# Computing the right half of row blocks 2 and 3 by Strassen while B streams in

## The chip, the cores and the metric

The kernel runs on one core of one Trainium2 chip. The metric is the device time of one execution in microseconds (us). All times are medians over several executions. The span that a profile gives is about 1.8 us shorter than the device time of the same execution, so spans are compared with spans and times with times.

Engine names: PE is the matrix engine, DVE the vector engine, ACT the scalar engine, POOL the GpSimd engine, SP the sync engine, which here only issues DMA transfers.

## The reference

```python
m, k, n = 2048, 2048, 2048           # a: m x k, b: k x n, gamma: n, all float32; eps = 1e-5

def reference(a, b, gamma, eps):
    x = np.matmul(a, b)
    rms = np.sqrt(np.mean(x ** 2, axis=-1, keepdims=True) + eps)
    return (gamma * x / rms).astype(np.float32)
```

A matrix product, then every row is divided by its root mean square and multiplied by gamma.

## The kernel before

The rows of A come in 16 blocks of 128. Row blocks 0 to 3 ("the head") are computed with plain bf16 matmuls while B streams in: a first stage for the left half of B's columns and a second stage for the right half. After that B stands in the core's memory, and groups of two row blocks follow: group g holds row blocks 2g and 2g+1, for g = 2 to 7. (The prediction calls g = 2 the first group; where a quoted expectation says third group, it is g = 3, with row blocks 6 and 7; g = 4 has row blocks 8 and 9.) A group has a left and a right half of the columns, and each half is one step of Strassen's method: seven products of 8 matmuls instead of eight. A product accumulates in a bank of PE's accumulation memory (the tile `acc`, 128 x 512 float32); ACT and DVE take the banks out and combine them.

There are eight tiles of 1024 float32 columns; the head fills all eight, and later row blocks reuse them, so a tile can be overwritten only when the store of the old row block has left it:

```python
x_slot = [consts.tile([P, HALF], FP32, name=f"x_{n}") for n in range(8)]
# ...
def x_tile(mb, h):
    if (mb, h) not in x_half:
        n = n_x[0]
        n_x[0] += 1
        if n < 8:
            slot = n
        else:
            g = n // 4
            slot = ((0, 4, 1, 5), (0, 1, 4, 5))[g // 2 % 2 == 0][n % 4] + 2 * (g % 2)
        x_half[mb, h] = x_slot[slot]
    return x_half[mb, h]
```

By this rule the left tile of row block 7 is tile 6, which held the right half of row block 2.

How a row block leaves: scaled in place by DVE, stored by SP, 512 KB per half.

```python
def finish(mb, order=(0, 1)):
    # ... (rms and its inverse)
    for h in order:
        x = x_half.pop((mb, h))
        nc.vector.scalar_tensor_tensor(
            out=x, in0=x, scalar=r, in1=gamma_sb[:, h * HALF:(h + 1) * HALF],
            op0=ALU.mult, op1=ALU.mult)
        nc.sync.dma_start(out=rows(mb, h * HALF, (h + 1) * HALF), in_=x)
```

Half a group, with "hooks" at which other work is put in, and the loads of the A blocks for the group after next. `t` is a scratch area that is only an alias of the result chunk `x22`, so the first ACT copy of a half writes into a tile that may still be on its way out:

```python
def group_half(g, j, hooks):
    # ...
    t = x22
    at_hook(0)
    p2, p5 = new_bank(), new_bank()
    product(g, j, 2, p2)
    c = spare if (g, j) == (G0, 0) else t        # G0 = 2
    nc.scalar.copy(out=c, in_=p2)
    last_squares()
    at_hook(1)
    product(g, j, 5, p5)
    nc.vector.tensor_tensor(out=t, in0=p5, in1=c, op=ALU.add)
    at_hook(2)
    p1 = new_bank()
    product(g, j, 1, p1)
    nc.vector.tensor_tensor(out=t, in0=p1, in1=t, op=ALU.subtract)
    at_hook(3)
    product(g, j, 4, p2, start=False)            # needs p2 copied out
    nc.scalar.copy(out=x21, in_=p2)
    # ... (products 3, 7, 6)

def load_after(g, mb):
    wait_for(x_chunk(2 * g + 1, 1)[:, 0:1])      # POOL reads one column, then issues
    load_block(mb)

def hooks_of(g, j):
    # ...
    if j == 0:
        if g == G0:
            # ...
            hook(2, finish, 1)
            hook(3, squares2, 2)
            hook(4, apply, nxt + 1)
            hook(4, finish, 2)                   # row block 2 leaves: LEFT half of g = 2
    else:
        # ...
        if g + 2 < NG:
            hook(0, load_after, g, nxt + 2)      # loads of blocks 2g+4, 2g+5: RIGHT half
            hook(0, load_block, nxt + 3)
            hook(5, row_norm, nxt + 2)
```

## Time and profile before

| | kernel before |
|---|---|
| device time, median | 224.48 us (three runs, 224.18 to 224.62) |
| span of the profiled execution | 222.6 us |
| PE busy | 211.1 us, 95% |
| PE waiting, all entries | 3.5 us, all before 24.7 us |
| one 512-column matmul, start to start | 215.8 ns |

From the page of the kernel before: the first line gives each engine's busy time, its share of the span and its number of instructions, the second each engine's share of the span in the chain of waits that ended last.

```profile
PE 211.1 (95%) x1043; PEld 98.6 (44%) x1043; DVE 161.8 (73%) x324; ACT 129.1 (58%) x272; POOL 24.5 (11%) x49
...
PE 83%; DMA 8%; DVE 2%; POOL 2%; issue 1%; ACT 1%; DVEq 0%; ACTq 0%; POOLq 0%
```

PE is the limit: followed back from the end, 83% of the span is PE's own work. The list of PE's waits in the kernel before (line, what it waited for, total us, times, longest us) has only four entries:

```profile
PE acc L138 <- DVE sq L129: 1.5, 1, 1.5
PE tbank L148 <- POOL msq L198: 1.2, 1, 1.2
PE acc L350 <- DMA b<-in_b_dram: 0.4, 1, 0.4
PE tbank L382 <- DVE head_at L170: 0.4, 1, 0.4
```

All lie at the start. So from 24.7 us on, PE never waits; a change gains only by taking matmuls away, and loses by every wait that it makes.

The timeline of PE in the kernel before, in the groups (start, duration, line, what, count). Line 279 is a Strassen product: 69.25 is the first product of group 2, 84.84 product 1 of its right half and 86.57 product 4.

```profile
69.25 3.62 PE L279 MATMUL acc<-b,s 128*128 128x512 bf16 x16
...
84.84 1.89 PE L279 MATMUL acc<-early,s 128*128 128x512 bf16 x8
86.57 3.77 PE L279 MATMUL acc<-early,at_even 128*128 128x512 bf16 x16
...
97.08 1.89 PE L279 MATMUL acc<-t_left,s 128*128 128x512 bf16 x8
98.81 3.62 PE L279 MATMUL acc<-t_left,head_at 128*128 128x512 bf16 x16
102.26 7.07 PE L279 MATMUL acc<-b,s 128*128 128x512 bf16 x32
```

No line carries a bracket, that is, no idle time before it. Next, when the A blocks 8 and 9 are asked for:

```profile
88.37 1.06 POOL L115 DMA_DIRECT2D a<-in_a_dram  x2 [0.32 <-issue]
```

### The profile page before, as it was taken

The page shows a single profiled execution, that of the slowest core. Times are in us where ns is not written, and L with a number is a line of the kernel's source. Part 1 is how long each engine was busy: PE and PEld are TensorE (multiplying, and loading weights), DVE is VectorE, ACT ScalarE, POOL GpSimd, SP SyncE. Part 2 cuts the span into 40 slices and gives each one's busy share as a digit, 9 for nine tenths or more (in the row PEclk, how much of TensorE's full clock was granted, in tenths as well). Part 3 has the DMA queues.
Part 4 walks back from the last instruction along what each step waited for, and adds up shares of the span by engine and source line. Part 5 has one row for each costly group of instructions (what it writes and reads, how often), then busy time and mean ns, then how long its engine had stood idle before and what let it go on. Part 6 is the DMA issues. An engine that isn't in the chain of part 4 may idle for free.

```text
span 222.6 us, 3026 instructions
## 1 busy us (share of the span) xinstructions
PE 211.1 (95%) x1043; PEld 98.6 (44%) x1043; DVE 161.8 (73%) x324; ACT 129.1 (58%) x272; POOL 24.5 (11%) x49
## 2 busy tenths in 40 slices
PE   7899999999999999999999999999999999999950
PEld 2445444444454444444444444444444444444430
DVE  2427557983999989978949298837994589587692
ACT  3110002807698895799646985699478954334570
POOL 7534232300000001000100002000200000000000
PEclk9999999999999999999999999999999999999997
DMA  6999999999973499818889259945994794044045
GB/s 184 223 202 209 203 208 211 212 303 259 327 280 159 188 272 292 310 72 226 276 228 400 58 174 222 366 151 143 246 368 168 97 282 189 0 188 193 0 190 188
DMA packets 36176, 47.13 MB, mean 212 GB/s; under 512 B 21952, under 2 KB 26048, under 8 KB 34496
## 3 DMA queue, kind: packets, MB, share of 16 engines
q0 software_dynamic: 9648, 23.33, 41.6%
q1 hardware_dynamic: 26080, 22.29, 33.0%
q10 hardware_dynamic: 432, 1.31, 2.0%
q8 instruction: 8, 0.13, 0.2%
q14 instruction: 8, 0.07, 0.1%
HBM read 34.60 MB, written 16.78 MB: 231 GB/s over the span
## 4 chain that ended last, share of the span: by engine, by line
PE 83%; DMA 8%; DVE 2%; POOL 2%; issue 1%; ACT 1%; DVEq 0%; ACTq 0%; POOLq 0%
PE acc L279 63%; PE acc L350 18%; DMA b<-in_b_dram 8%; POOL early L106 1%; DVE x L617 1%; POOL b L100 1%; DVE x L620 1%; PE tbank L179 1%; PE tbank L382 1%; PE tbank L165 1%; ACT sq L291 0%; DVEq L732 0%; ACT sq L682 0%; DVE x L690 0%; DVE r L322 0%
## 5 line engine op out<-in xcount | busy, mean ns | idle before, releaser
L279 PE MATMUL acc<-b,s 128*128 128x512 bf16 x376 | 83.3, 379 | 0.0
L279 PEld LDWEIGHTS <-s 128*128 128x128 f16 x472 | 46.2, 98 | 55.7 <-DVE s L244 0.2
L350 PE MATMUL acc<-b,head_at 128*128 128x512 bf16 x240 | 55.1, 379 | 0.6 <-DMA b<-in_b_dram 0.4
L291 ACT ACTIVATE sq<-x 128x512 bf16<-128x512 f32 x62 | 39.1, 631 | 10.9 <-DVE x L520 5.1
L340 DVE SCALAR_TENSOR_TENSOR x<-x,r,gamma_sb 128x1024 f32<-128x1024 f32 x28 | 34.7, 1282 | 0.8
L209 ACT ACTIVATE sq<-a 128x1024 bf16<-128x1024 f32 x24 | 25.4, 1057 | 16.8 <-DMA a<-in_a_dram 16.4
L350 PEld LDWEIGHTS <-head_at 128*128 128x128 bf16 x240 | 22.9, 98 | 26.7 <-issue 1.1
L393 ACT COPY x<-acc 128x512 f32<-128x512 f32 x11 | 5.9, 591 | 25.1 <-PE acc L350 25.1
L231 ACT ACTIVATE head_at<-a,s 128x2048 f16<-128x2048 f32 x10 | 19.9, 1990 | 0.0
L279 PEld LDWEIGHTS <-at_even 128*128 128x128 f16 x96 | 9.4, 98 | 11.5 <-issue 0.4
L279 PEld LDWEIGHTS <-head_at 128*128 128x128 f16 x96 | 9.4, 98 | 11.3
L100 POOL DMA_DIRECT2D b<-in_b_dram x15 | 10.6, 708 | 16.0 <-DMA b<-in_b_dram 13.2
L217 DVE TENSOR_SCALAR s<-norm 128x1 f32<-128x1 f32 x12 | 1.8, 150 | 14.3 <-ACT norm L212 14.2
L244 DVE TENSOR_TENSOR s<-at_even 128x1024 f16<-128x1024 f16 x15 | 9.7, 684 | 2.8 <-DMA at_even<-head_at 2.8
L291 ACT ACTIVATION_READ_ACCUMULATOR sq<-x 128x1 f32 x62 | 11.7, 188 | 0.0
L279 PE MATMUL acc<-t_left,s 128*128 128x512 bf16 x48 | 11.3, 379 | 0.0
L279 PE MATMUL acc<-early,s 128*128 128x512 bf16 x48 | 11.3, 379 | 0.0
L279 PE MATMUL acc<-early,at_even 128*128 128x512 bf16 x48 | 11.0, 379 | 0.0
L279 PE MATMUL acc<-t_left,at_even 128*128 128x512 bf16 x48 | 10.9, 379 | 0.0
L509 ACT COPY x<-acc 128x512 f32<-128x512 f32 x10 | 5.7, 575 | 8.9 <-PE acc L279 8.9
L279 PE MATMUL acc<-t_left,head_at 128*128 128x512 bf16 x48 | 10.8, 379 | 0.0
L279 PE MATMUL acc<-early,head_at 128*128 128x512 bf16 x48 | 10.8, 379 | 0.0
(86 smaller groups left out, 205.8 us busy)
## 6 DMA issues: line engine op xcount, KB each, us to landing
out_dram<-x SPq DMA_DIRECT2D x30, 512.0 KB, 3.1
a<-in_a_dram POOLq DMA_DIRECT2D x12, 1024.0 KB, 8.5
b<-in_b_dram POOLq DMA_DIRECT2D x15, 512.0 KB, 17.1
early<-in_a_dram POOLq DMA_DIRECT2D x7, 256.0 KB, 14.8
early<-in_b_dram ACTq DMA_DIRECT2D x2, 512.0 KB, 5.9
gamma_sb<-in_gamma_dram POOLq DMA_DIRECT2D x1, 1024.0 KB, 19.9
out_dram<-x SPq DMA_DIRECT2D x3, 256.0 KB, 3.5
early<-in_a_dram SPq DMA_DIRECT2D x1, 512.0 KB, 5.7
```

The costliest lines, as they stand in the source:

```text
L100: nc.gpsimd.dma_start(out=raw[j][kp], in_=b[kp * W2:(kp + 1) * W2, j * HALF:(j + 1) * HALF].rearrange("(t p) n -> p t n", p=P))
L106: nc.gpsimd.dma_start(out=ah(kp), in_=a[0:HB * P, kp * W2:(kp + 1) * W2].rearrange("(r p) k -> p r k", p=P))
L165: nc.tensor.matmul(view[:, t, r, :], ah(kp)[:, r, t * P:(t + 1) * P], identity, is_transpose=True, start=(t == 0 and r == 0), stop=(t == 1 ...
L209: nc.scalar.activation(out=junk, in_=a32[mb][:, h * HALF:(h + 1) * HALF], func=ACTF.Square, scale=2.0 ** -8, accum_out=n2[:, h:h + 1])
L231: nc.scalar.activation(out=a16[mb], in_=a32.pop(mb), func=ACTF.Copy, scale=factor.pop(mb))
L244: nc.vector.tensor_tensor(out=s_sum[s], in0=x, in1=y, op=op)
L279: nc.tensor.matmul(bank, lhsT[:, kp, :], rhs, start=(start and kp == 0), stop=(kp == KP - 1), skip_group_check=not start)
L291: nc.scalar.activation(out=sq[:, 0:CH], in_=src, func=ACTF.Square, scale=inv_sqrt_n, accum_out=msq[mb][:, c:c + 1])
L340: nc.vector.scalar_tensor_tensor(out=x, in0=x, scalar=r, in1=gamma_sb[:, h * HALF:(h + 1) * HALF], op0=ALU.mult, op1=ALU.mult)
L350: nc.tensor.matmul(bank, head_at[:, kt, r, :], head_rhs(c, kt), start=(kt == 0), stop=(kt == KT - 1))
L393: copy(out=x_chunk(*g), in_=banks[g])
L509: nc.scalar.copy(out=x21, in_=p2)
```

## The change

Intent: the right half of row blocks 2 and 3 is also done by Strassen ("the pair"), with its products 2, 5 and 1 accumulated while B's right half streams in. That is 56 matmuls for 64. To make room, A blocks 4 and 5 are no longer transposed within the second stage and after it, but at the end of the pair. The first group gets a new order: row block 0 is scaled in two parts, row block 1 and blocks 6 and 7 come at other hooks. The end of the pair adds operations on row blocks 2 and 3 in group 2's left half, so their squares move behind, and the scaling and storing of row block 2 moves to the right half. The core of the diff:

```diff
+    spare = [spare[:, 0:CH], consts.tile([P, CH], FP32, name="t_first")]
...
+    def stream_right(kp):
+        order = [(g, kt) for kt in (2 * kp, 2 * kp + 1) for g in plain]   # row blocks 0, 1
...
+        if kp < KP - 1:
+            for m in (2, 5):
+                pair_matmul(m, kp)                                        # the pair: 2, 3
+            if kp > 0:
+                pair_matmul(1, kp - 1)
...
+    product(PAIR, 1, 4, pair[2], start=False)
...
+    product(PAIR, 1, 3, pair[5], start=False)
...
+    product(PAIR, 1, 7, p7, within={5: [lambda: turn(HB, 0)]})
...
+    product(PAIR, 1, 6, p6)
...
@@ group_half
-        t = x22
+        first = (g, j) == (G0, 0)
+        c, t = (spare if first else (spare[1], spare[1])) if g == G0 else (x22, x22)
...
@@ load_after
-        wait_for(x_chunk(2 * g + 1, 1)[:, 0:1])
+        wait_for(at(2 * g + 3)[:, KT - 1, 0:1] if g == G0 else x_chunk(2 * g + 1, 1)[:, 0:1])
...
@@ hooks_of, left half, g == G0
-                hook(0, row_factor, nxt)
-                hook(1, row_norm, nxt + 1)
-                hook(1, apply, nxt)
+                hook(0, finish, 0, (1,))
+                hook(1, row_norm, nxt)
+                hook(1, take_rms, 1)
+                hook(2, row_factor, nxt)
+                hook(2, finish, 0, (0,))
+                hook(2, apply, nxt)
+                hook(2, row_norm, nxt + 1)
                 hook(2, a_sums, g, (7, 6))
+                hook(2, finish, 1, (1, 0))
                 hook(2, row_factor, nxt + 1)
-                hook(2, finish, 1)
-                hook(3, squares2, 2)
+                hook(2, pair_sums)
+                hook(2, pair_ends)
                 hook(4, apply, nxt + 1)
-                hook(4, finish, 2)
-                hook(6, b_sum_7, 1, KP - 1)
+                hook(5, square_half, r2, 1)
+                hook(5, take_rms, r2)
+                hook(5, square_half, r3, 1)
@@ hooks_of, right half, g == G0
-                hook(1, squares2, r3)
-                for kp in range(KP):
-                    hook(2, b_sum_6, 1, kp)
+                hook(2, finish, r2)
```

In the changed kernel the scratch area of group 2 is `t_first`, a tile of its own; from group 3 on it is `x22`, as before.

More of the change, by code (lines that the diff above doesn't have):

```diff
@@ L50 @@
     sq_pool = ctx.enter_context(tc.tile_pool(name="sq_pool", bufs=1))
-    stat_pool = ctx.enter_context(tc.tile_pool(name="stat_pool", bufs=8))
+    stat_pool = ctx.enter_context(tc.tile_pool(name="stat_pool", bufs=4))
+    msq_pool = ctx.enter_context(tc.tile_pool(name="msq_pool", bufs=8))
     ps_t = ctx.enter_context(tc.tile_pool(name="ps_t", bufs=1, space=bass.MemoryType.PSUM))
@@ L75 @@
     x_slot = [consts.tile([P, HALF], FP32, name=f"x_{n}") for n in range(8)]
-    spare = head_at.rearrange("p t r m -> p (t r m)")[:, K:2 * K].bitcast(FP32)[:, 0:CH]
+    spare = head_at.rearrange("p t r m -> p (t r m)")[:, K:2 * K].bitcast(FP32)
+    spare = [spare[:, 0:CH], consts.tile([P, CH], FP32, name="t_first")]
     def a16_slot(mb):
-        if mb < HB + 2:
-            return x_slot[HB + 1 + 2 * (mb % 2)].bitcast(FP16)
         flat = head_at.rearrange("p t r m -> p (t r m)").bitcast(FP16)
@@ L111, with load_half @@
     a32 = {}
+    def load_half(mb, h):
+        if h == 0:
+            a32[mb] = a_pool.tile([P, K], FP32, name="a32")
+        nc.gpsimd.dma_start(out=a32[mb][:, h * HALF:(h + 1) * HALF],
+                            in_=a[mb * P:(mb + 1) * P, h * HALF:(h + 1) * HALF])
     def load_block(mb):
@@ L123 @@
     load_head(1)
-    identity_f = consts.tile([P, P], FP32, name="identity_f")
+    identity_f = t_left[:, 2, KP - 1, 0:2 * P].bitcast(FP32)
     make_identity(nc, identity_f)
@@ L129 @@
     nc.vector.memset(warm, 0.0)
+    nc.vector.memset(pace, 1.0)
+    nc.scalar.activation(out=pace, in_=pace, func=ACTF.Sqrt)
     identity = consts.tile([P, P], BF16, name="identity")
@@ L172, with transpose_half @@
     a16 = {}
-    def transpose_half(mb, g):
-        bank = ps_t.tile([P, CH], FP32, name="tbank")
+    def transpose_half(mb, g, own_bank):
+        if own_bank:
+            bank = ps_t.tile([P, CH], FP32, name="tbank")
+        else:
+            bank = ps_a.tile([P, CH], FP32, name="acc")
         view = bank.bitcast(FP16).rearrange("p (g m) -> p g m", m=P)
@@ L182, in transpose_half, with take_transposed @@
             )
-        nc.vector.tensor_copy(out=at(mb)[:, g * 8:(g + 1) * 8, :], in_=view)
+        return view
+    def take_transposed(mb, g, view, copy):
+        copy(out=at(mb)[:, g * 8:(g + 1) * 8, :], in_=view)
     def transpose_dma(mb):
@@ L192, in new_msq @@
     def new_msq(mb):
-        msq[mb] = stat_pool.tile([P, NCH + 1], FP32, name="msq")
+        msq[mb] = msq_pool.tile([P, NCH + 1], FP32, name="msq")
         n_sq[mb] = 0
@@ L197 @@
         new_msq(mb)
+        nc.gpsimd.memset(msq[mb][:, NCH - 1:NCH], 0.0)
         nc.gpsimd.memset(msq[mb][:, NCH:], float(eps))
@@ L235, in quarter, with sum_of, a_sums @@
     def quarter(g, r, c):
+        if g < G0:
+            return head_at[:, c::2, 2 * g + r, :]
         return at(2 * g + r)[:, c::2, :]
-    def a_sums(g, which):
+    def sum_of(g, s):
+        return s_sum[s].bitcast(BF16) if g < G0 else s_sum[s]
+    def a_sums(g, which, lo=0, hi=KP):
         a11, a12, a21, a22 = (quarter(g, r, c) for r in range(2) for c in range(2))
@@ L243, in a_sums @@
             x, y, op = terms[s]
-            nc.vector.tensor_tensor(out=s_sum[s], in0=x, in1=y, op=op)
+            nc.vector.tensor_tensor(out=sum_of(g, s)[:, lo:hi, :], in0=x[:, lo:hi, :],
+                                    in1=y[:, lo:hi, :], op=op)
     def b_quarter(j, kp, r, c):
@@ L254, in b_sums @@
             nc.vector.tensor_tensor(out=sums[j][:, n, kp, :], in0=x, in1=y, op=op)
-    def b_sum_7(j, kp):
-        b21, b22 = (b_quarter(j, kp, 1, c) for c in range(2))
-        nc.vector.tensor_tensor(out=b21, in0=b21, in1=b22, op=ALU.add)
-    def b_sum_6(j, kp):
-        b11, b12 = (b_quarter(j, kp, 0, c) for c in range(2))
-        nc.vector.tensor_tensor(out=b12, in0=b12, in1=b11, op=ALU.add)
     def b_sums_in_place(j, kp):
@@ L270, in b_sums_in_place, with product_matmul, product @@
                                 op=ALU.add)
-    def product(g, j, m, bank, start=True):
-        for kp in range(KP):
-            lhsT = {3: quarter(g, 0, 0), 4: quarter(g, 1, 1)}[m] if m in (3, 4) else s_sum[m]
-            rhs = {1: lambda: sums[j][:, 0, kp, :], 2: lambda: b_quarter(j, kp, 0, 0),
-                   3: lambda: sums[j][:, 1, kp, :], 4: lambda: sums[j][:, 2, kp, :],
-                   5: lambda: b_quarter(j, kp, 1, 1), 6: lambda: b_quarter(j, kp, 0, 1),
-                   7: lambda: b_quarter(j, kp, 1, 0)}[m]()
-            nc.tensor.matmul(bank, lhsT[:, kp, :], rhs,
-                             start=(start and kp == 0), stop=(kp == KP - 1),
-                             skip_group_check=not start)
+    def product_matmul(g, j, m, bank, kp, start=True):
+        lhsT = {3: quarter(g, 0, 0), 4: quarter(g, 1, 1)}[m] if m in (3, 4) else sum_of(g, m)
+        rhs = {1: lambda: sums[j][:, 0, kp, :], 2: lambda: b_quarter(j, kp, 0, 0),
+               3: lambda: sums[j][:, 1, kp, :], 4: lambda: sums[j][:, 2, kp, :],
+               5: lambda: b_quarter(j, kp, 1, 1), 6: lambda: b_quarter(j, kp, 0, 1),
+               7: lambda: b_quarter(j, kp, 1, 0)}[m]()
+        nc.tensor.matmul(bank, lhsT[:, kp, :], rhs,
+                         start=(start and kp == 0), stop=(kp == KP - 1),
+                         skip_group_check=not start)
+    def product(g, j, m, bank, start=True, within={}):
+        for kp in range(KP):
+            for work in within.get(kp, ()):
+                work()
+            product_matmul(g, j, m, bank, kp, start)
     x_half = {}
@@ L291, in square, with square_half @@
         nc.scalar.activation(out=sq[:, 0:CH], in_=src, func=ACTF.Square,
+                             scale=inv_sqrt_n, accum_out=msq[mb][:, c:c + 1])
+    def square_half(mb, h):
+        c = n_sq[mb]
+        n_sq[mb] += 1
+        sq = sq_pool.tile([P, 2 * CH], BF16, name="sq")
+        nc.scalar.activation(out=sq, in_=x_tile(mb, h), func=ACTF.Square,
                              scale=inv_sqrt_n, accum_out=msq[mb][:, c:c + 1])
@@ L332, in rows @@
         return out[mb * P:(mb + 1) * P, lo:hi]
+    inverse_of = {}
     def finish(mb, order=(0, 1)):
-        if mb not in rms_of:
-            take_rms(mb)
-        r = inverse(rms_of.pop(mb))
+        if mb not in inverse_of:
+            if mb not in rms_of:
+                take_rms(mb)
+            inverse_of[mb] = inverse(rms_of.pop(mb))
+        r = inverse_of[mb]
         for h in order:
@@ L354, in new_bank @@
         return ps_a.tile([P, CH], FP32, name="acc")
-    later = ([("b", kp) for kp in range(5)]
-             + [("a", HB), ("b", 5), ("b", 6), ("a", HB + 1), ("b", 7)])
+    later = [("b", kp) for kp in range(KP)] + [("a", n) for n in range(4)]
     def load_later(n):
@@ L361, in load_later @@
             kind, which = later.pop(0)
-            load_b(1, which) if kind == "b" else load_block(which)
+            load_b(1, which) if kind == "b" else load_half(HB + which // 2, which % 2)
     def stream(groups, kp, before=(), when=None):
@@ L393, in evict @@
             copy(out=x_chunk(*g), in_=banks[g])
+    PAIR = G0 - 1
     groups1 = [(r, c) for r in range(HB) for c in range(2)][:-1]
@@ L399 @@
         x_tile(r, 0)
+    early_sums = {4: ((2,), 0, 6), 5: ((5,), 0, 7), 6: ((1,), 0, KP)}
     transpose_first()
@@ L406 @@
         before = [lambda: transpose_head(kp + 1)] if kp + 1 < KP else []
+        if kp in early_sums:
+            before.append(lambda: a_sums(PAIR, *early_sums[kp]))
         stream(groups1, kp, before, len(groups1) + 5 if kp == 0 else None)
@@ L412 @@
             b_sums(0, kp - 1)
+        if 0 < kp < KP - 2:
+            b_sums_in_place(0, kp - 1)
     load_later(2)
-    b_sums(0, KP - 1)
-    def prepare(mb):
-        row_norm(mb)
-        row_factor(mb)
-        row_apply(mb)
-    def b_sums_2(kp):
-        b_sums_in_place(0, kp)
-        b_sums(1, kp)
-        if kp + 1 < KP:
-            b_sum_7(1, kp)
-    r3 = HB - 1
-    squares = groups1 + [last1]
-    groups2 = [(r, c) for r in range(HB) for c in (2, 3)][:-1]
+    squares = groups1 + [last1]
@@ new lines, with pair_matmul @@
+    plain = [(r, c) for r in range(2) for c in (2, 3)]
+    pair = {}
+    def pair_matmul(m, kp):
+        if kp == 0:
+            pair[m] = new_bank()
+        product_matmul(PAIR, 1, m, pair[m], kp)
+    def stream_right(kp):
+        order = [(g, kt) for kt in (2 * kp, 2 * kp + 1) for g in plain]
+        if kp in (0, KP - 1):
+            order.sort(key=lambda x: plain.index(x[0]))
+        if kp == KP - 1:
+            for m in (2, 5):
+                pair_matmul(m, kp)
+            pair_matmul(1, kp - 1)
+        for g, kt in order:
+            if kt == 0:
+                banks[g] = new_bank()
+            head_matmul(banks[g], *g, kt)
+        if kp < KP - 1:
+            for m in (2, 5):
+                pair_matmul(m, kp)
+            if kp > 0:
+                pair_matmul(1, kp - 1)
+        else:
+            pair_matmul(1, kp)
@@ L431 @@
     for kp in range(KP):
         load_later(1)
-        before = [lambda: transpose_half(HB, 0)] if kp == 6 else []
-        if kp == 7:
-            before = [lambda: transpose_half(HB, 1)]
-        stream(groups2, kp, before)
+        b_sums(1, kp)
+        stream_right(kp)
         square(squares[kp][0], x_chunk(*squares[kp]))
-        if kp == 4:
-            prepare(HB)
-        if kp == 6:
-            prepare(HB + 1)
-        elif kp == KP - 1:
-            b_sums_in_place(0, kp - 1)
-        else:
-            b_sums_2(kp)
+        if kp > 0:
+            b_sums_in_place(1, kp - 1)
@@ L447 @@
+        if kp == 0:
+            b_sums(0, KP - 1)
+            b_sums_in_place(0, KP - 3)
+        if kp == 1:
+            b_sums_in_place(0, KP - 2)
+            b_sums_in_place(0, KP - 1)
+        if kp == 2:
+            a_sums(PAIR, (2,), 6, KP)
+            a_sums(PAIR, (5,), 7, KP)
+        if kp in (3, 4):
+            a_sums(PAIR, ((7, 6)[kp - 3],))
     nc.gpsimd.dma_start(out=gamma_sb, in_=gamma.partition_broadcast(P))
@@ L449, with turn, pair_sums, pair_ends @@
     load_block(HB + 3)
-    def squares2(r):
-        for c in (2, 3):
-            square(r, x_chunk(r, c))
-    evict(groups2[0:2], ())
-    squares2(0)
-    evict(groups2[2:-1], ())
-    bank = new_bank()
-    for kt in range(KT):
-        if kt in (0, 6):
-            transpose_half(HB + 1, kt // 6)
-            if kt == 0:
-                b_sums(1, KP - 2)
-                b_sum_7(1, KP - 2)
-        head_matmul(bank, r3, 3, kt)
-    evict(groups2[-1:], ())
-    row_norm(HB + 2)
-    a_sums(G0, (2, 5, 1))
-    finish(0, (1, 0))
-    b_sums_2(KP - 1)
-    nc.scalar.copy(out=x_chunk(r3, 3), in_=bank)
-    squares2(1)
+    r2, r3 = HB - 2, HB - 1
+    for r in range(HB):
+        x_tile(r, 1)
+    x11, x12, x21, x22 = (x_chunk(r, c) for r in (r2, r3) for c in (2, 3))
+    nc.scalar.copy(out=x22, in_=pair[2])
+    nc.vector.tensor_tensor(out=x22, in0=pair[5], in1=x22, op=ALU.add)
+    evict(plain, (2, 3))
+    b_sums_in_place(1, KP - 1)
+    product(PAIR, 1, 4, pair[2], start=False)
+    row_norm(HB)
+    row_norm(HB + 1)
+    nc.vector.tensor_tensor(out=x22, in0=pair[1], in1=x22, op=ALU.subtract)
+    row_factor(HB)
+    product(PAIR, 1, 3, pair[5], start=False)
+    row_apply(HB)
+    nc.scalar.copy(out=x21, in_=pair[2])
+    row_factor(HB + 1)
+    row_apply(HB + 1)
+    p7 = new_bank()
+    turned = {}
+    def turn(mb, g):
+        turned[mb, g] = transpose_half(mb, g, g == 0)
+    product(PAIR, 1, 7, p7, within={5: [lambda: turn(HB, 0)]})
+    turn(HB, 1)
+    for g in range(2):
+        take_transposed(HB, g, turned[HB, g], nc.scalar.copy)
+    nc.scalar.copy(out=x12, in_=pair[5])
+    p6 = new_bank()
+    product(PAIR, 1, 6, p6)
+    a_sums(G0, (5,))
+    for g in range(2):
+        turn(HB + 1, g)
+        take_transposed(HB + 1, g, turned[HB + 1, g], nc.vector.tensor_copy)
+    square_half(0, 1)
+    square_half(1, 1)
+    take_rms(0)
+    a_sums(G0, (2, 1))
+    def pair_sums():
+        nc.vector.tensor_tensor(out=x11, in0=x22, in1=x21, op=ALU.add)
+        nc.vector.tensor_tensor(out=x22, in0=x22, in1=x12, op=ALU.add)
+    def pair_ends():
+        nc.vector.tensor_tensor(out=x11, in0=p7, in1=x11, op=ALU.add)
+        nc.vector.tensor_tensor(out=x22, in0=p6, in1=x22, op=ALU.add)
     late = []
@@ L491, in group_half @@
         x11, x12, x21, x22 = (x_chunk(ra, c1), x_chunk(ra, c2), x_chunk(rb, c1), x_chunk(rb, c2))
-        t = x22
+        first = (g, j) == (G0, 0)
+        c, t = (spare if first else (spare[1], spare[1])) if g == G0 else (x22, x22)
         at_hook(0)
         p2, p5 = new_bank(), new_bank()
-        product(g, j, 2, p2)
-        c = spare if (g, j) == (G0, 0) else t
-        nc.scalar.copy(out=c, in_=p2)
+        one, two = ((5, p5), (2, p2)) if first else ((2, p2), (5, p5))
+        product(g, j, *one)
+        nc.scalar.copy(out=c, in_=one[1])
         last_squares()
         at_hook(1)
-        product(g, j, 5, p5)
-        nc.vector.tensor_tensor(out=t, in0=p5, in1=c, op=ALU.add)
+        product(g, j, *two)
+        nc.vector.tensor_tensor(out=t, in0=two[1], in1=c, op=ALU.add)
         at_hook(2)
```

## The prediction

> **What bounds it now.** The matrix engine. The page gives PE 95% busy; the chain of waits is PE for 83% of the span and, from 24.7 to 209.5 us, nothing but PE: PE's list of waits holds four, 3.5 us together, all before 24.7 us. A 512-column matmul costs 215.8 ns (91 in 19.64 us in the chain). The Trainium skill, "TensorE: Matmul & The Clock Gate", section "Wait — 56ns, not 53.3ns?", states 215.7 ns start to start when warm; the trace agrees. Only fewer matmuls shorten the middle; every new PE wait lengthens it.
>
> **Removed.** Right half of row blocks 2 and 3: 64 matmuls become 7 products of 8 = 56. 8 x 0.216 = 1.73 us, all on the critical path. Transposes and later groups keep their work. The 1.28 us table load before the first Sqrt on ACT (timeline, 53.6 us) moves to the start.
>
> **Added.** On DVE 5 sums of A (0.68 us each) and 6 combining operations (0.69 us). On ACT wide squares replace pairs.
>
> **Where new waits may come**, from the instruction order per engine and trace durations:
> - First B stage: 0.6 us of in-place sums per step fits DVE's gaps (0.26 + 1.25 us per 3.9 us step). No wait.
> - Second stage: a step shrinks from 3.02 to 2.38 us, while B tiles land every 2.5 us. From issue-to-landing times, with the A blocks moved behind, the last right tiles land at about 51.0, 53.5, 55.9; PE asks at 51.5, 53.9, 56.3. Margins shrink to 0.3 us: 0 to 0.5 us lost.
> - End of the pair: scaling block 4 writes where products 4 and 3 read, so it starts after product 3 (about 62.5) and takes 1.28 us; its transposes, placed after 5 matmuls of product 7, wait about 0.4 us. Groups then start about 68.35 instead of 69.25 us.
> - First group: before the copy that frees product 2's bank in the right half, ACT must do norm 6, apply 6 (1.9), norm 7, two copies with squares, apply 7 and two wide squares: done about 86.5 us by my sum, while PE wants it for product 4 at 85.7. Estimate: 0.8 us wait, uncertain by 1 us. Product 7 needs its A sum at 78.8 (ready about 76.2); product 5 of the right half needs the pair's product 7 read by 82.2 (ready about 81.9).
> - Later groups: same code, loads starting near the same time (87.5 against 88.4 us). This should hold.
>
> **Sum.** -1.73 + 0.4 + 0.8 (0 to 1.8) + 0.2 = about -0.3 us; as the first group's waits may be smaller, -0.6 us: 223.9 us, 8 in 10 within 222.8 to 225.4. Without waits it is 222.75. Faster by over 2%: 0.02; within 2%: 0.96; slower by over 2%: 0.02.
>
> **What would show it.** 8 fewer PE matmuls; first-group products starting 0.5 to 1.7 us before 69.25 us; new entries in PE's waits: block 4's transposes on the DVE scaling (about 0.4 us), product 4 of the first group's right half on an ACT copy (0 to 2 us), second-stage matmuls on B's DMA (0 to 0.5 us). Then PE without gaps and the same 13 us tail.
>
> **What would make it wrong.** B landing later; DVE sums delaying the transposed-A copies; block 6 or 7 landing late so that norm, factor, apply, transpose pushes into later groups; ACT copies of 1024 columns, which this trace does not have, being far over 1 us.

## More of the kernel before

The timelines of SP, POOL and ACT in the kernel before:

```profile
84.70 1.64 SPq L343 DMA_DIRECT2D out_dram<-x  x2
```

```profile
96.49 0.57 ACT L498 COPY x<-acc 128x512 f32<-128x512 f32 x1
...
98.34 1.99 ACT L231 ACTIVATE head_at<-a,s 128x2048 f16<-128x2048 f32 x1
```

The two stores of row block 2 are issued at 84.70 us, 3.7 us before the loads. The copy at 96.49 us is the first of group 3, which overwrites tile 6; it runs without a wait. The line at 98.34 us is the scaling of A block 8 for group 4. And the DMA view of the kernel before for the stretch in which the stores were issued (count, size each, median us from issue to landing):

```profile
out_dram<-x SPq DMA_DIRECT2D x2, 512.0 KB, 3.7
```

## The result, and the profile after

| | before | changed |
|---|---|---|
| device time, median (4 runs each) | 224.52 us | 226.88 us |
| lowest to highest | 224.18 to 224.62 | 226.00 to 226.95 |
| span of the profiled execution | 222.6 us | 225.2 us |
| PE busy | 211.1 us | 210.1 us |
| PE matmuls on record | 1043 | 1015 |
| PE weight loads on record (PEld) | 1043 | 1035 |

The changed kernel is slower by 1.0%: the ratio is 1.0103, with a 95% interval of 1.0084 to 1.0122. A ratio here is the mean time of one kernel's fast runs over that of the other's of the same rounds, so it is not quite the ratio of the medians that are quoted. The time is outside the predicted range, and on the other side of the kernel before.

The page of the changed kernel, the same two lines as of before:

```profile
PE 210.1 (93%) x1015; PEld 97.9 (43%) x1035; DVE 168.0 (75%) x330; ACT 127.7 (57%) x263; POOL 25.7 (11%) x55
...
PE 37%; DVE 6%; DMA 4%; ACT 1%; issue 1%; DVEq 0%; ACTq 0%
```

PE has less work, as intended: the weight loads, one for each matmul, fell by the 8 that the change takes away. (The matmul records fell by 28; 20 of them are missing from this trace, so some counts below are 15 or 31 where the kernel has 16 or 32.) The shares of the second line add up to about half: this chain can be followed back only to 107.2 us, so its 37% can't be set against the 83% of before. What it does show is that, followed back from the end, it leaves PE at 127.2 us, in group 4, and goes through DVE, ACT and DMA. The list of PE's waits in the changed kernel tells where they are:

```profile
PE acc L289 <- ACT x L571: 1.9, 1, 1.9
PE acc L145 <- DVE pace L135: 1.5, 1, 1.5
PE acc L289 <- ACT t_first L571: 0.7, 1, 0.7
PE acc L289 <- DVE s L264: 0.7, 1, 0.7
PE tbank L408 <- DVE head_at L177: 0.3, 1, 0.3
PE acc L377 <- DMA b<-in_b_dram: 0.3, 1, 0.3
PE acc L289 <- DVE x L575: 0.3, 1, 0.3
```

The four entries at line 289, 3.6 us together, are waits of Strassen products, where the kernel before had none. The timeline of PE in the changed kernel places them (the bracket is the idle time before the line and what ended it):

```profile
67.33 3.73 PE L289 MATMUL acc<-b,s 128*128 128x512 bf16 x15
...
82.99 1.89 PE L289 MATMUL acc<-early,s 128*128 128x512 bf16 x8
85.61 3.61 PE L289 MATMUL acc<-early,at_even 128*128 128x512 bf16 x16 [0.73 <-ACT t_first L571]
...
95.97 1.89 PE L289 MATMUL acc<-t_left,s 128*128 128x512 bf16 x8
99.76 1.89 PE L289 MATMUL acc<-t_left,head_at 128*128 128x512 bf16 x8 [1.90 <-ACT x L571]
101.94 1.89 PE L289 MATMUL acc<-t_left,head_at 128*128 128x512 bf16 x8 [0.30 <-DVE x L575]
103.66 7.07 PE L289 MATMUL acc<-b,s 128*128 128x512 bf16 x31
...
120.04 3.63 PE L289 MATMUL acc<-b,s 128*128 128x512 bf16 x16 [0.67 <-DVE s L264]
```

Setting starts of the same product against each other gives a ledger of the whole change:

| PE starts | before | changed | shift |
|---|---|---|---|
| group 2, first product | 69.25 | 67.33 | -1.92 |
| group 2, right half, product 1 | 84.84 | 82.99 | -1.85 |
| group 2, right half, product 4 | 86.57 | 85.61 | -0.96 |
| group 3, left half, product 1 | 97.08 | 95.97 | -1.11 |
| group 3, left half, product 4 | 98.81 | 99.76 | +0.95 |
| group 3, left half, product 7 | 102.26 | 103.66 | +1.40 |
| last product of the kernel | 212.77 | 215.28 | +2.51 |

The pair brought its whole 1.9 us. Group 2 then lost 0.89, group 3 lost 2.51 (from -1.11 to +1.40) and group 4 lost 1.11 (from +1.40 to +2.51). The sum of what came after the pair is 4.43 us, and 3.62 us of it lies in groups 3 and 4. Each column is one profiled execution. In the profiles of the eight kernels with the changed start (the changed kernel and all experiments but 4), group 2 began between 67.33 and 67.97 us, so the -1.92 is uncertain by up to 0.6 us; the losses within the groups, read from differences inside one profile, are not touched by that.

What did product 4 of group 3 wait for? For the copy that frees its bank. The timeline of ACT in the changed kernel:

```profile
99.12 0.59 ACT L571 COPY x<-acc 128x512 f32<-128x512 f32 x1 [5.21 <-DMA out_dram<-x]
...
100.99 1.99 ACT L246 ACTIVATE head_at<-a,s 128x2048 f16<-128x2048 f32 x1
```

ACT stood still for 5.21 us before that copy, until a store of results (`out_dram<-x`) had landed: the copy writes tile 6, and row block 2's right half was still leaving it. Before, the same copy ran at 96.49 us. The scalings of A blocks 8 and 9, which stand behind it on ACT, moved from 98.34 to 100.99 us and from 104.30 to 106.94; their transposes, and with them the sums of A for group 4, come later by about as much (the DVE timelines have the sums at 116.41 before and 119.29 after, in both cases when a transposing DMA has landed), and PE waits 0.67 us for them at 120.04.

And why was the store still under way? The timelines of SP and of POOL in the changed kernel:

```profile
87.70 1.53 SPq L370 DMA_DIRECT2D out_dram<-x  x2
```

```profile
85.84 1.05 POOL L120 DMA_DIRECT2D a<-in_a_dram  x2 [0.34 <-ACT t_first L571]
```

The stores are issued 3.0 us later than before and the loads of blocks 8 and 9 2.5 us earlier, so their order is turned round: 2 MB of loads now stand ahead of 1 MB of stores. The DMA view of the changed kernel, first for 88 to 92 us, then for 92 to 98 us (packets, MB, share of the 16 DMA engines; the software queue q0 carries POOL's loads, the hardware queue q1 SP's stores; the last line is the landing time of the two stores):

```profile
q0 software_dynamic: 191, 1.43, 98.5%
...
out_dram<-x SPq DMA_DIRECT2D x2, 512.0 KB, 10.1
```

```profile
q1 hardware_dynamic: 284, 1.04, 42.6%
q0 software_dynamic: 79, 0.52, 27.1%
```

Between 88 and 92 us the stores' queue moved nothing. Their whole megabyte went out after 92 us, and they took 10.1 us to land in place of 3.7 us. The DMA instructions on SP look as short as before, 1.53 us from the start of the first to the end of the second (0.33 us each); the Trainium skill, "Perfetto Trace Analysis", section "Summary: the profiler window per engine type", says that the reported window of such an instruction leaves out the data movement, and this trace agrees: 0.33 us on SP against 10.1 us to landing.

### The profile page after: what moved, and what is told of

Read it like the earlier page. It is cut to its first block, busy times and chain, and to the rows that moved or that the text cites. A ratio compares the mean times of both kernels' runs of the same rounds, so it can differ in the third digit from the quotient of the medians.

```text
span 225.2 us, 2994 instructions
## 1 busy us (share of the span) xinstructions
PE 210.1 (93%) x1015; PEld 97.9 (43%) x1035; DVE 168.0 (75%) x330; ACT 127.7 (57%) x263; POOL 25.7 (11%) x55
## 5 line engine op out<-in xcount | busy, mean ns | idle before, releaser
L289 PE MATMUL acc<-b,s 128*128 128x512 bf16 x397 | 91.7, 379 | 1.3 <-DVE s L264 0.7
L289 PEld LDWEIGHTS <-s 128*128 128x128 f16 (+1 forms) x512 | 49.8, 98 | 60.8 <-DVE s L264 1.6
L377 PE MATMUL acc<-b,head_at 128*128 128x512 bf16 x171 | 41.2, 379 | 0.6 <-DMA b<-in_b_dram 0.3
L307 ACT ACTIVATE sq<-x 128x512 bf16<-128x512 f32 x54 | 34.1, 632 | 9.3 <-DVE x L593 3.7
L377 PEld LDWEIGHTS <-head_at 128*128 128x128 bf16 x176 | 16.8, 98 | 19.7 <-issue 0.6
L289 PEld LDWEIGHTS <-head_at 128*128 128x128 f16 (+1 forms) x112 | 10.9, 98 | 15.8 <-issue 2.8
L419 ACT COPY x<-acc 128x512 f32<-128x512 f32 x6 | 3.4, 588 | 24.8 <-PE acc L377 24.8
L289 PE MATMUL acc<-early,head_at 128*128 128x512 bf16 x63 | 14.4, 379 | 0.1
L264 DVE TENSOR_TENSOR s<-head_at 128x1024 f16<-128x1024 f16 (+5 forms) x22 | 13.5, 639 | 0.1
L280 DVE TENSOR_TENSOR b<-b 128x1024 bf16<-128x1024 bf16 x16 | 10.9, 693 | 0.2
```

The lines of the kernel that those rows point to most:

```text
L264: nc.vector.tensor_tensor(out=sum_of(g, s)[:, lo:hi, :], in0=x[:, lo:hi, :], in1=y[:, lo:hi, :], op=op)
L280: nc.vector.tensor_tensor(out=flat[:, 1:3, :], in0=flat[:, 1:3, :], in1=flat[:, 0::3, :], op=ALU.add)
L289: nc.tensor.matmul(bank, lhsT[:, kp, :], rhs, start=(start and kp == 0), stop=(kp == KP - 1), skip_group_check=not start)
L307: nc.scalar.activation(out=sq[:, 0:CH], in_=src, func=ACTF.Square, scale=inv_sqrt_n, accum_out=msq[mb][:, c:c + 1])
L377: nc.tensor.matmul(bank, head_at[:, kt, r, :], head_rhs(c, kt), start=(kt == 0), stop=(kt == KT - 1))
L419: copy(out=x_chunk(*g), in_=banks[g])
```

## The experiments

The theory (A in the quoted texts): row block 2's stores now stand behind the loads of blocks 8 and 9, land late, and hold back the first copy of group 3, since that copy's scratch area is the tile that the store still reads; ACT hands the delay on to PE and, through the scalings of blocks 8 and 9, to group 4. The rivals: that the delay is born in group 2, where ACT's new wide squares make PE wait 0.7 us and shift what follows; and that the new order of the loads, or the Strassen pair as such, is to blame, and not the reuse of the tile. The letters other than A in the quoted texts stand for these rivals as each text puts them. Experiments 1 to 4 ran on one chip (kernel before there: 224.34 us), 5 to 8 on another (224.40 us). The changed kernel was not run again on these chips: the ratios below compare with the kernel before in the same rounds, and differences from the changed kernel's 226.88 us, measured earlier, are good to about 0.2 us, by which the kernel before differed. All gave the right result. The name in brackets is the one that the quoted texts use for a run; no run is called e7. Each diff is against the changed kernel, but for experiment 4.

### 1. Loads behind the stores (e1_loads_behind)

```diff
-        wait_for(at(2 * g + 3)[:, KT - 1, 0:1] if g == G0 else x_chunk(...)[:, 0:1])
+        wait_for(x_slot[r2 + HB][:, 0:1] if g == G0 else x_chunk(...)[:, 0:1])
...
-                hook(0, load_after, g, nxt + 2)
-                hook(0, load_block, nxt + 3)
+                at_n = 2 if g == G0 else 0
+                hook(at_n, load_after, g, nxt + 2)
+                hook(at_n, load_block, nxt + 3)
```

> The changed kernel, with the loads of row blocks 8 and 9 held until row block 2 has been scaled, so that its two stores are issued first. Theory A (the stores of row block 2 are issued 2 us after 2 MB of loads, share the DMA engines with them and land after 10.1 us instead of about 3.5; the copy of product 2 in the next group overwrites that tile and waits for the store, and PE, then the scaling of block 8 and the sums of group 4 wait for that copy): stores land within 4 us, the 5.2 us wait of ACT for a store is gone, PE's two waits in the third group (1.9 and 0.3 us) are gone and that of 0.7 us before group 4 shrinks: 223.3 to 224.3 us, ratio to the changed kernel 0.985 to 0.99. Rival B (ACT simply has too much work in the first groups, whatever the stores do): unchanged, 226.9 us. Rival C (it is the loads of blocks 8 and 9 and the transposes behind them that are late for group 4): 3.5 us later loads make it worse, over 228 us.

Measured: 228.19 us (227.74 to 228.76), ratio 1.0161 (1.0138 to 1.0184). The stores landed in 2.7 us, and ACT's wait for a store was gone. But the kernel got slower than the changed one: the time alone fits rival C of the quoted text (over 228 us) and not A. The timeline of ACT in this run:

```profile
98.29 1.06 ACT L223 ACTIVATE sq<-a 128x1024 bf16<-128x1024 f32 x1 [7.06 <-DMA a<-in_a_dram]
...
100.85 0.56 ACT L571 COPY x<-acc 128x512 f32<-128x512 f32 x1
```

The loads were issued at 90.09 us and now landed late; the norm of block 8 waited 7.06 us for them, and it stands ahead of group 3's first copy in ACT's order. The copy came at 100.85 us, later still, and PE waited 3.0 us for it. The Trainium skill, "TensorE: Matmul & The Clock Gate", in the specification table at its top, calls ScalarE's queue a strict FIFO; this run agrees: the copy, with its bank full and its tile free, did not pass the waiting norm. What follows: the store's delay is due to the order behind the loads, but putting both loads behind the stores only changes which of the two ACT waits for. The time that theory A was given here was wrong, because ACT's order had not been looked at. This run alone does not decide between A and C; experiments 2 and 4 do.

### 2. The scratch area of group 3's left half in a tile of its own (e2_own_scratch)

```diff
-        c, t = (spare if first else (spare[1], spare[1])) if g == G0 else (x22, x22)
+        own = g == G0 or (g, j) == (G0 + 1, 0)
+        c, t = (spare if first else (spare[1], spare[1])) if own else (x22, x22)
```

> The changed kernel, with the loads where they are, but the running sum of the left half of the third group kept in the scratch tile that the group before uses, not in the tile whose store is under way. Theory A: the stores still take about 10 us to land, but the copy of product 2 no longer waits for them; PE's waits in the third group go or fall to under 0.5 us in all, block 8 is scaled about 2.5 us earlier and the sums of group 4 are in time: 223.3 to 224.3 us. Rival B (too much work on ACT): unchanged, 226.9 us. Rival D (what hurts is the crowding of the DMA engines itself, not the reuse of the tile): unchanged or nearly, over 226 us.

Measured: 223.42 us (223.35 to 223.64), ratio 0.9957 (0.9942 to 0.9972): 3.5 us below the changed kernel, and faster than the kernel before. The order of loads and stores is untouched, and the stores still took 9.1 us to land; only nobody waits for them. From the DMA view and the timelines of ACT and PE in this run:

```profile
out_dram<-x SPq DMA_DIRECT2D x2, 512.0 KB, 9.1
```

```profile
94.90 0.58 ACT L572 COPY t_first<-acc 128x512 f32<-128x512 f32 x1 [0.70 <-DVE x L599]
```

```profile
98.03 3.62 PE L289 MATMUL acc<-t_left,head_at 128*128 128x512 bf16 x16
```

The copy now comes at 94.90 us in place of 99.12, after 0.70 us for DVE, which still read `t_first`, and without a wait for a store. PE's waits in groups 3 and 4 are gone, and product 4 of group 3 starts at 98.03 us without a gap. Of the waits of Strassen products only the 0.7 us in group 2 is left. This is the experiment that decides for A: here the late stores cost nothing once the copy no longer wrote their tile. It also shows that group 4's wait was only handed on from group 3.

### 3. Row block 3's wide square out of ACT's way in group 2 (e3_square_later)

```diff
@@ left half, g == G0
-                hook(5, square_half, r3, 1)
@@ right half, g == G0
+                hook(1, square_half, r3, 1)
```

> The changed kernel, with the wide square of row block 3 moved behind the copy that frees product 2's bank in the right half of the first group. The 0.9 us gap of PE there is gone in every theory. Theory A: PE then comes 0.9 us earlier to the third group, but the tile is freed by the DMA, about the same time as before, so the wait there grows by most of what was won: 226.2 to 226.9 us. Rival B (ACT's load): the 0.9 us and more is kept, at most 226.0 us.

Measured: 226.46 us (226.26 to 226.57), ratio 1.0090 (1.0075 to 1.0105). The wait of 0.7 us in group 2 stayed, against the expectation. The copy that PE waits for still came at 84.98 us: it writes `t_first`, and DVE's last operation of the left half (line 598 of the changed kernel) reads `t_first` until 84.89 us. So the wait has a second cause that ends at the same time, which this edit does not touch. Group 3's waits stayed too (4.7 us on ACT for the store, 1.4 us on PE), so they do not come from these squares.

### 4. The kernel before, with row block 2 stored late (e4_before_late_store)

Row block 2 is scaled where the kernel before scales it, but its stores are issued in group 2's right half, after five of the eight B sums there.

```diff
-                hook(4, finish, 2)
+                hook(4, scale_only, 2)
...
                 for kp in range(KP):
                     hook(2, b_sum_6, 1, kp)
+                    if kp == 4:
+                        hook(2, store_late, 2)
```

(`scale_only` and `store_late` are the two parts of `finish`; the second rewrites one column on DVE so that the stores wait for that place.)

> The kernel before, with one thing of the change put in alone: row block 2 is scaled where it was, but its two stores are issued only after the loads of blocks 8 and 9 (a rewrite of one column, 0.15 us each, holds them until about 90 us). Theory A: the stores land after 8 to 10 us, at about 99 us, the copy of product 2 in the third group waits for them about 3 us, PE waits 1 to 2 us there and up to 1 us before group 4: 225.7 to 227.5 us against 224.5. Rivals B and C: no change, 224.4 to 224.8 us.

Measured: 227.76 us (227.49 to 228.07), ratio 1.0149 (1.0132 to 1.0167), slightly above the expected range. The stores were issued at 89.91 us, behind the loads at 88.11 us, and took 9.4 us. The timeline of ACT in this run, and its list of PE's waits:

```profile
100.19 0.58 ACT L516 COPY x<-acc 128x512 f32<-128x512 f32 x1 [4.07 <-DMA out_dram<-x]
```

```profile
PE acc L279 <- ACT x L516: 2.1, 1, 2.1
...
PE acc L279 <- DVE s L244: 1.0, 1, 1.0
PE acc L279 <- DVE x L520: 0.5, 1, 0.5
```

These are the changed kernel's three waits in groups 3 and 4, in a kernel with no Strassen pair. 3.6 us of new PE waits stand against 3.4 us of added time. So the late store alone is enough, and the pair is not to blame.

### 5. Both causes of group 2's wait taken away, and group 3's (e5_free_bank)

Group 2's right half uses its own result chunk as scratch (a tile that row block 1 leaves in the left half), group 3's left half uses `t_first`, and the square moves as in experiment 3.

```diff
-        c, t = (spare if first else (spare[1], spare[1])) if g == G0 else (x22, x22)
+        c, t = (spare if first else
+                (spare[1], spare[1]) if (g, j) == (G0 + 1, 0) else (x22, x22))
@@ left half, g == G0
-                hook(5, square_half, r3, 1)
@@ right half, g == G0
+                hook(1, square_half, r3, 1)
```

> The changed kernel with three small moves: the third group's left half keeps its running sum in the free scratch (as in e2), the right half of the first group keeps its own in the tile it writes anyway (the store of row block 1 from it landed at about 81.6 us), and the wide square of row block 3 comes after the copy that frees product 2's bank. Theory A, made more exact by e3 (the 0.9 us gap of PE in the first group had two causes ending within 0.1 us of each other: two wide squares on ACT ahead of the copy, and the scratch still read by DVE until 84.9 us): the gap falls from 0.9 to under 0.2 us and nothing later eats it, 222.3 to 222.8 us, ratio to the kernel before 0.990 to 0.993. If the gap had one cause only, e6 shows the same as this one.

Measured: 222.57 us (222.50 to 222.86), ratio 0.9921 (0.9908 to 0.9935): the fastest of all, 4.3 us below the changed kernel and 1.8 us below the kernel before. Its whole list of PE's waits:

```profile
PE acc L145 <- DVE pace L135: 1.5, 1, 1.5
PE acc L377 <- DMA b<-in_b_dram: 0.4, 1, 0.4
PE tbank L408 <- DVE head_at L177: 0.4, 1, 0.4
PE tbank L155 <- POOL msq L212: 0.3, 1, 0.3
```

No Strassen product waits any more, though the stores of row block 2 still took 9.4 us.

### 6. The same tiles as in 5, without moving the square (e6_own_tile_only)

```diff
-        c, t = (spare if first else (spare[1], spare[1])) if g == G0 else (x22, x22)
+        c, t = (spare if first else
+                (spare[1], spare[1]) if (g, j) == (G0 + 1, 0) else (x22, x22))
```

> As e5 without the move of the square: the copy no longer waits for the scratch, but stands behind both wide squares on ACT. Two causes: the gap of 0.7 us (0.9 with the pipeline) in the first group stays, 223.3 to 223.6 us, as e2. One cause, the scratch: gap gone, 222.3 to 222.8 us as e5.

Measured: 223.51 us (223.16 to 223.80), ratio 0.9957 (0.9943 to 0.9970). Group 2's wait is 0.6 us. With experiments 3 and 5 this settles that wait: moving the square alone leaves 0.7 us, another tile alone leaves 0.6 us, both leave none. It has two causes that end within 0.1 us of each other, ACT's squares and DVE's read of `t_first`.

### 7. Only block 9's load behind the stores (e8_block9_behind)

```diff
-                hook(0, load_block, nxt + 3)
+                if g == G0:
+                    hook(2, wait_for, x_slot[r2 + HB][:, 0:1])
+                hook(2 if g == G0 else 0, load_block, nxt + 3)
```

> The changed kernel with the load of row block 9 alone held until row block 2 has been scaled (about 89 us); that of block 8 stays at 85.8 us, so only 1 MB of loads stands before the stores. Theory A (stores and loads share the DMA engines; 3 MB take 10 us): the stores land after about 6 us, near 95 us, the copy of product 2 in the third group waits about 1 us for them instead of 5.2, PE does not wait there, the sums of group 4 are in time as block 9 is not needed before 99 us: 223.3 to 224.0 us. If the stores are late for another reason than the loads ahead of them: still about 10 us, 226.5 to 227 us.

Measured: 223.56 us (223.27 to 223.98), ratio 0.9964 (0.9951 to 0.9976). With one megabyte ahead of them the stores landed in 5.4 us (median of the two):

```profile
out_dram<-x SPq DMA_DIRECT2D x2, 512.0 KB, 5.4
```

ACT waited 0.7 us for the store in place of 5.2, PE not at all in groups 3 and 4. So in these three runs the delay grows with the loads ahead: 2.7 us with none (experiment 1), 5.4 us with one block, 10.1 us with two; experiment 8 shows that their amount is not all. This is the other cure, by order instead of by tile, and it gives nearly the same: 3.3 us below the changed kernel, where experiment 2 gave 3.5.

### 8. Experiments 5 and 7 together (e9_all)

The edit is that of 5 and that of 7.

> e5 and e8 together. Theory A: the store is no longer in anybody's way in e5, so moving the load of block 9 adds nothing: equal to e5 within 0.3 us, 222.3 to 222.9 us; later only if block 9 comes late for its norm.

Measured: 223.13 us (222.76 to 223.27), ratio 0.9941 (0.9928 to 0.9953). The two cures do not add: once nobody waits for the store, its order is worth nothing. By the medians it is 0.6 us slower than experiment 5, outside the expected 0.3 us, though the intervals of the two still overlap. The two profiled executions differ by only 0.1 us in all. In that of this run, group 2 began at 67.42 us, 0.38 us earlier than in experiment 5, so the longer wait of PE for POOL at the start (1.1 us against 0.3) cost nothing there. Group 4 then lost this lead and 0.1 us more: block 8 was scaled at 97.28 us in place of 96.32, the sums of A for group 4 began at 115.52 in place of 114.60, and PE waited 0.2 us for them.

The landing time is a surprise. One block stands ahead of the stores, as in experiment 7, and yet they took 7.4 and 9.8 us:

```profile
out_dram<-x SPq DMA_DIRECT2D x2, 512.0 KB, 8.6
```

The stores were issued 1.1 us after block 8's load here and 1.9 us after it there, and their last 0.15 MB, from 94 us on, went out beside the load of block 9, which was issued after both. So the amount of loads ahead does not by itself set the landing time; what else does was not tested.

## Why the prediction was wrong

- **Held: the gain of the pair.** "8 x 0.216 = 1.73 us, all on the critical path." Group 2 began 1.92 us earlier: 1.68 of it from the start of the second stage on, against 1.73 by the count of matmuls, and 0.24 because that stage already began at 39.60 instead of 39.84 us, which the change does not explain. The Trainium skill's 215.7 ns per warm matmul, cited in the prediction with its page, again matched the trace (215.9 ns: 56 matmuls in 12.09 us from 135.86 us on, in the changed kernel).
- **Held, and better than put: the second stage and the turning of block 4.** 0 to 0.5 us and 0.4 us of waits were predicted, "Groups then start about 68.35"; neither wait came, and group 2 started at 67.33. PE ran from 39.60 us to 62 us without a gap, and the scaling of block 4 began on DVE at 61.82 us, in time for its transposes at 63.16.
- **Held: group 2.** "Estimate: 0.8 us wait, uncertain by 1 us." It was 0.73 us in the trace, 0.89 us in the ledger. But the reason was half: besides ACT's squares there was the scratch tile that DVE reads (experiments 3, 5 and 6), and that the second cause added nothing to the size was luck.
- **Failed: "Later groups: same code, loads starting near the same time (87.5 against 88.4 us). This should hold."** The term was set to about zero and measured +3.62 us: 2.51 in group 3 and 1.11 in group 4. The code of the later groups is indeed the same, but what they wait for is not: the store of row block 2, issued behind the loads, still held the tile that group 3's first copy writes, and ACT stood 5.21 us for it. I looked at when the loads start, and not at where row block 2's stores stand relative to them. `finish` of row block 2 had moved by 3.0 us, the loads by 2.5 us the other way (at 85.84 us, not at my estimated 87.5), and the tile reuse that had always been there became a wait.

With that term left out, the ledger gives 224.52 - 1.92 + 0.07 + 0.89 - 0.15 = 223.4 us, that is 1.1 us below the kernel before; experiment 2, which takes away just that term, measured 223.42 us, 0.9 us below the kernel before on its chip. That the two times agree so closely is luck, given the 0.2 us between chips and the spread of the starts. The prediction's "Without waits it is 222.75" met 222.57 us in experiment 5. So the sum was otherwise close, with two predicted waits that did not come, and the one term set to zero is what put the result outside the range. The prediction's own list of what could go wrong named block 6 or 7 landing late, the B tiles, DVE's sums and ACT's long copies (which took 1.01 us, as hoped), and no store at all.

What stays open: why the DMA engines served the loads so long before the first byte of the stores, and why one block of loads ahead cost 5.4 us in experiment 7 and 8.6 us in experiment 8. The traces show that it was so, not by which rule.

## What to carry to other kernels

When a change moves a store, ask which later instruction overwrites the stored tile, and which loads will now be issued ahead of it: in these runs two stores of 512 KB landed in 2.7 us with no loads ahead and in 9.1 to 10.3 us with 2 MB ahead, and an instruction stream that overwrites the tile inherits that. Before moving transfers to cure such a wait, look for another place for the scratch data; a tile that no transfer touches cured it whole here, while holding both loads back made the next instruction of the same engine wait instead. Where two waits end at the same time, removing one shows nothing, so test both alone and together before one is acquitted.

## What the Trainium skill lacked or had wrong

- "DMA: Bandwidth & Descriptors", sections "Issuing engines are not separate DMA queues" and "Queues, rings and completion order": the first says that transfers from the scalar, sync and gpsimd engines run on the same 16 DMA engines and interleave, the second that each DMA engine takes turns between the queue rows that it has work for, packet by packet. Sharing is what the trace shows; taking turns is not, at first. In the changed kernel, with stores issued at 87.70 us, POOL's queue moved 1.43 MB from 88 to 92 us and SP's nothing; without loads ahead (experiment 1) SP's queue had already moved 0.35 MB by 90 us after an issue at 88.33. The two queues moved data side by side only later (0.40 and 0.15 MB from 92 to 94 us). The trace does not show when the stores' descriptors reached the DMA engines, so this says that the stores got no turn for about 4 us, not why; for what a kernel sees, the measurement decides.
- The same page gives bandwidth and first-byte latency, but no landing time for a transfer behind others. The runs show, for two stores of 512 KB: 2.7 us with no loads ahead, 5.4 and 8.6 us with 1 MB ahead (experiments 7 and 8), 9.1 to 10.3 us with 2 MB.
- "Perfetto Trace Analysis", section "Optimization Strategy", says to find the gaps on the engine in question and the semaphore or semaphores that it waits for. It does not warn that a cause may have a twin that ends at the same time, so that removing one shows nothing: in group 2 two causes ended within 0.1 us, and removing either alone left 0.6 or 0.7 us of a 0.7 us gap (experiments 3 and 6).
- None of the pages cited here says that reusing an on-chip tile as scratch while its store is in flight puts a compute engine behind the DMA queues: ACT stood 5.2 us before a copy of 0.6 us.
